# Two-part products of 256 columns merged into 512 in eight feed-forward blocks, with reordered gates in a recurrent block

## The chip, the cores and the metric

The program runs on one core of one Trainium2 chip. The metric is device time in microseconds (us) from start to end of one execution. The kernel before took 2142.56 us (median of 3 runs, 2142.15 to 2143.3).

## The reference

Thirteen blocks follow one another on a residual stream x of 256 tokens by 1024 features, batch 1: eight SwiGLU feed-forward blocks (half weight in the residual for all), one HGRN2 recurrent block, one forgetting attention, one short convolution, one shared key/value block and one sparse attention. Everything is float32. What bears on the change:

```python
def swiglu(h, w_in, w_out):                     # D_FF = 2816, eight times
    gate, up = jnp.split(h @ w_in, 2, axis=-1)
    return (jax.nn.silu(gate) * up) @ w_out

def hgrn2_mixer(h, w_in, lb, out_norm_g, w_out):
    q, z_f, i, g = jnp.split(h @ w_in, 4, axis=-1)
    f = lb + (1.0 - lb) * jax.nn.sigmoid(z32)
    k = (1.0 - lb) * jax.nn.sigmoid(-z32)
    q = jax.nn.silu(q)
    ...                                          # o: gated linear recurrence over q, k, f, v
    o = rmsnorm(o, out_norm_g).reshape(B, T, D_MODEL)
    o = o * jax.nn.silu(g)
    return o @ w_out

def short_conv_mixer(x, w_in, conv_w, w_out):
    b_gate, c_gate, v = jnp.split(x @ w_in, 3, axis=-1)
    ...                                          # y: causal convolution of c_gate * v, width 3
    return (b_gate * y) @ w_out
```

## The kernel before, in words

**Products.** Each float32 number is split in two parts of a shorter type (float32r): a high part h and a rest l. A product w·x is then wh·xh + wh·xl + wl·xh: three matmuls, each with its own load of 128x128 weights and 256 moving columns (`mm_w`, or `mm_x` where the activations are the weights). `proj` makes one product of the stream with one piece of weights: 1024 features to 256, that is 2 halves of 128 outputs by 8 steps of 128 features by 3 matmuls, 48 in all. Its two halves share one PSUM bank, which is read as 128x512. `proj_out` is the product back to the stream, also 48 matmuls, into four accumulating banks.

**Weights.** Pieces of 1 MB arrive by DMA on SP's queue into four buffers, in the order of `plan()`. `prep` casts a quarter of a piece to its high part on ScalarE (line 177) and subtracts it on VectorE for the low part (line 179); the quarters named in `pool_parts` are subtracted on GpSimd instead.

**Order.** Everything is emitted in an order written out by hand. A model clock `self.t` advances with each matmul by a fixed cost; `tick()` then emits a quarter of `prep` each `pace`, and runs a step of any background generator whose due time has come (`spawn`, `yield 3600.0`). `finish(task)` emits what remains of a generator at once. The engines execute in emission order and wait on semaphores.

**A feed-forward block** (`ffn`) has 11 units: gate product, up product, then the output product of the unit before. The gate's bank is scaled by the norm's factor on VectorE (line 477), then Silu on ScalarE (479), scaling on GpSimd (480), times the up product on VectorE (484), split into ah and al (487, 488). The first unit interleaves gate and up over the 8 feature steps (`outer`), while the previous block's last results arrive, and the norm's factor is computed in it (`stats`); `spread` then broadcasts the factor with two matmuls from dg (line 444) and a copy to rb (line 453). Only in the very first block does another product (`ahead`) stand ahead of `spread`. PSUM has 8 banks: a ring P of four for products and the other four for accumulation; in the block after the key/value block (site 10) P has three.

**The recurrent block** (`hg`) has four passes of products q, z and v; each spawns `levels`, which runs seven levels: matmuls of kk and qs into a bank, an update of qs on VectorE (568) and of kk on GpSimd (569), then a masked copy on VectorE (575). After the four passes come four gate products, then four output products. `levels` ends with a norm (squares on ScalarE, an 11-instruction root on 4 columns on VectorE, lines 414 to 425) and writes `on` (599); `gated` multiplies it on GpSimd and transposes it. From the third pass on, a pass first finishes the task of two passes before. Quarters 1 and 3 of each piece are subtracted on GpSimd.

**Convolution and tables.** In the convolution, each pass has products b, c and v in ring P. `tables` (attention bias tables for a later block: five small matmuls, two PSUM copies and DMAs on GpSimd's queue, 3 MB to DRAM) runs in the background of the third block, with banks from ring P.

Of the kernel before, what the change touches and what calls it, by code (L numbers as in the profile page):

```python
# [71 lines left out]
def plan(phases=PHASES):  # L72
# [10 lines left out]
    for ph in phases:  # L83
# [8 lines left out]
        elif ph[0] == "hg":  # L92
            for p in range(4):
                pieces += [("hg_w_in", (0,), "in", block(4 * s + p)) for s in range(3)]
            pieces += [("hg_w_in", (0,), "in", block(12 + p)) for p in range(4)]
            pieces += [("hg_w_out", (0,), "out", block(p)) for p in range(4)]
        elif ph[0] == "fox":
            pieces += [("fox_w_in", (0,), "in", block(0)), ("fox_w_in", (0,), "in", block(4))]
            pieces.append(("fox_w_in", (0,), "in", range(4096, 4112)))
            pieces.append(("fox_w_in", (0,), "in", block(8)))  # L100
            for p in range(1, 4):
                pieces += [("fox_w_in", (0,), "in", block(4 * s + p)) for s in range(3)]
            pieces += [("fox_w_in", (0,), "in", block(12 + p)) for p in range(4)]
# [15 lines left out]
class Builder:  # L119
# [154 lines left out]
    def proj(self, kinds, xs, outer=False, stats=None):  # L274
# [31 lines left out]
        return banks  # L306

    def mini(self, n, xs, ring=None):

# [35 lines left out]
    def begin_site(self, site):  # L345
        pl = self.kvx if site == 9 and self.kvx else self.act
        self.site = site
        self.xs = (
            pl.tile([128, 8, 256], F32R, name="xh", tag="xh", bufs=1),
            pl.tile([128, 8, 256], F32R, name="xl", tag="xl", bufs=1),  # L350
        )
        self.ssum = self.sm.tile([128, 512], F32, name="ssum", tag="ssum", bufs=1)
# [106 lines left out]
    def ffn(self, nxt):  # L459
        nc, tc = self.nc, self.tc  # L460
        A = self.comp(self.P + self.aside)
        xs = self.xs
        with tc.tile_pool(name="ffn", bufs=2, reuse_waits="tile") as pl:
            acc = prev = ahead = None
            for u in range(NU):
                if u == 0 and self.site != 10:
                    begin = self.use_i == 0
# [8 lines left out]
                g1 = pl.tile([128, 2, 256], F32, name="g1", tag="g1")  # L476
# [6 lines left out]
                av = pl.tile([128, 2, 256], F32, name="av", tag="av")  # L483
                nc.vector.tensor_tensor(av, banks[1].rearrange("p (c t) -> p c t", c=2), sg, op=ALU.mult)  # L484
                ah = pl.tile([128, 2, 256], F32R, name="ah", tag="ah")
# [39 lines left out]
    def hg(self, nxt):  # L525
# [3 lines left out]
        with tc.tile_pool(name="hg", bufs=2, reuse_waits="tile") as pl:  # L529
            masks = pl.tile([128, 576], F32, name="masks", tag="masks", bufs=1)  # L530
            nc.scalar.dma_start(masks, self.a["M"])
            lb8, oml = self.lb8, self.oml
            self.pool_parts = (1, 3)
            scs = [pl.tile([128, 6, 128], F32, name=f"sc{i}", tag=f"sc{i}", bufs=1) for i in range(2)]
            for s in scs:
                nc.gpsimd.memset(s, 0.0)
            on = pl.tile([128, 2, 1024], F32, name="on", tag="on", bufs=1)
            paces = (3600.0, 3600.0, 3600.0, 3000.0)
            tiles = [(j, h) for j in range(2) for h in range(2)]

            def levels(p, qs, kk, ff, v):
# [57 lines left out]
                nc.vector.tensor_tensor(  # L599
                    on[:, :, 256 * p:256 * p + 256].rearrange("p j (h d) -> p j h d", h=2),  # L600
                    o.rearrange("p (j h d) -> p j h d", j=2, h=2),
                    rs.rearrange("p (j h) -> p j h", j=2)[:, :, :, None].to_broadcast([128, 2, 2, 128]),
                    op=ALU.mult,
                )
# [7 lines left out]
            tasks = []  # L612
            for p in range(4):
                if p == 0:
                    bq, bz = self.proj("ww", xs, outer=True, stats=lambda: self.stats(True))
                    self.spread()
                else:
                    (bq,) = self.proj("w", xs)
# [20 lines left out]
                (bv,) = self.proj("x", xs)  # L639
# [4 lines left out]
            gn = self.rows[:, R_GN:R_GN + 128]  # L644
            zs, zt = {}, []
            for p in range(4):
                (bg,) = self.proj("x", xs)
                gs = pl.tile([128, 2, 256], F32, name="gs", tag="gs", bufs=3)
                for j in range(2):
                    bj = bg[:, 256 * j:256 * j + 256]  # L650
                    nc.scalar.activation(gs[:, j], bj, AF.Silu, scale=self.rn[:, j:j + 1])
                g4 = gs.rearrange("p j (h d) -> p (j h) d", h=2)
                nc.gpsimd.tensor_tensor(g4, g4, gn[:, None, :].to_broadcast([128, 4, 128]), op=ALU.mult)
                zt.append(self.spawn(gated(p, gs, zs), 1500.0))

            def z(j):
                self.finish(zt[j])
                return zs[j]
# [48 lines left out]
    def fox(self, nxt):  # L707
# [6 lines left out]
        with tc.tile_pool(name="fox", bufs=2, reuse_waits="tile") as pl:  # L714
# [6 lines left out]
            def forget(turn):  # L721
# [172 lines left out]
    def conv(self, nxt):  # L894
        nc, tc = self.nc, self.tc
        xs = self.xs
        with tc.tile_pool(name="conv", bufs=2, reuse_waits="tile") as pl:
# [4 lines left out]
            for p in range(4):  # L902
                if p == 0:
                    bb, bc = self.proj("ww", xs, outer=True, stats=lambda: self.stats(True))
                    self.spread()
                else:
                    (bb,) = self.proj("w", xs)
# [6 lines left out]
                nc.vector.tensor_tensor(c1, bc.rearrange("p (c t) -> p c t", c=2), self.rb2(), op=ALU.mult)  # L914
                (bv,) = self.proj("w", xs)
                nc.vector.tensor_tensor(v1, bv.rearrange("p (c t) -> p c t", c=2), self.rb2(), op=ALU.mult)
# [16 lines left out]
    def tables(self, pl):  # L933
# [15 lines left out]
        b = self.bank(self.P)  # L949
        for q in range(4):  # L950
# [407 lines left out]
    def run(self):  # L1358
        nc, tc = self.nc, self.tc
        ph = self.phases  # L1360
        with tc.manual_schedule():
# [206 lines left out]
```

## Time and profile before

| | |
|---|---|
| median of 3 runs | 2142.56 us |
| profiled execution, its own time | 2140.52 us |
| its span (first to last instruction) | 2138.4 us |
| mean granted TensorE clock | 0.994 of full |
| TensorE (PE) busy | 2087.5 us, 98%, 17,299 matmuls |
| VectorE (DVE) busy | 1419.4 us, 66% |
| ScalarE (ACT) busy | 1027.9 us, 48% |
| GpSimd (POOL) busy | 401.4 us, 19% |
| DMA | 368.93 MB, mean 173 GB/s |

Busy time of a matmul runs to a modelled end and overlaps the next matmul's, so a busy PE says that it did not wait, and the distance from one start to the next says how fast it went. PE is the matmul itself, PEld its weight load. By the ends of the residual additions (line 392) the first feed-forward block ends at 203.6 us, the recurrent block at 385.4, and the other blocks at 577.1, 767.6, 925.8 (forgetting attention), 1116.2, 1306.0, 1399.0 (convolution), 1589.4, then key/value and the block after it 1823.0, sparse attention 1945.2, and the last at 2135.0.

### The profile page before, as it was taken

The page shows a single profiled execution, that of the slowest core. Times are in us where ns is not written, and L with a number is a line of the kernel's source. Part 1 is how long each engine was busy: PE and PEld are TensorE (multiplying, and loading weights), DVE is VectorE, ACT ScalarE, POOL GpSimd, SP SyncE. Part 2 cuts the span into 40 slices and gives each one's busy share as a digit, 9 for nine tenths or more (in the row PEclk, how much of TensorE's full clock was granted, in tenths as well). Part 3 has the DMA queues.
Part 4 walks back from the last instruction along what each step waited for, and adds up shares of the span by engine and source line. Part 5 has one row for each costly group of instructions (what it writes and reads, how often), then busy time and mean ns, then how long its engine had stood idle before and what let it go on. Part 6 is the DMA issues. An engine that isn't in the chain of part 4 may idle for free.

```text
span 2138.4 us, 41531 instructions
## 1 busy us (share of the span) xinstructions
PE 2087.5 (98%) x17299; PEld 2064.0 (97%) x17299; DVE 1419.4 (66%) x2566; ACT 1027.9 (48%) x2076; POOL 401.4 (19%) x357
## 2 busy tenths in 40 slices
PE   8999889999999998999999999999999999999999
PEld 7999889999999998999999999999999999879999
DVE  7656776756666578575667657775578665687554
ACT  5544434544444456654454445454445444565442
POOL 2002646300100023320010001110021100442000
PEclk9999999999999999999999999999999999999999
DMA  7554423595455545345545554555546554223551
GB/s 264 199 191 149 158 80 122 181 238 196 152 205 190 175 158 183 133 175 200 178 158 207 188 179 156 200 193 181 186 174 228 179 185 170 97 101 131 211 190 60
DMA packets 57020, 368.93 MB, mean 173 GB/s; under 512 B 6318, under 2 KB 10694, under 8 KB 14080
## 3 DMA queue, kind: packets, MB, share of 16 engines
q1 hardware_dynamic: 53600, 355.49, 46.3%
q0 software_dynamic: 2656, 10.07, 2.5%
q8 instruction: 135, 2.21, 0.4%
q10 hardware_dynamic: 576, 0.72, 0.1%
q14 instruction: 53, 0.43, 0.1%
HBM read 360.75 MB, written 4.46 MB: 171 GB/s over the span
## 4 chain that ended last, share of the span: by engine, by line
PE 72%; DVE 6%; ACT 2%; issue 1%; POOL 0%; DMA 0%; DVEq 0%; ACTq 0%
PE b L245 71%; DVE wl L179 2%; PE b L250 1%; DVE xl L360 1%; ACT wh L177 1%; DVE x L392 1%; DVE rs_t L423 0%; DVE rs_t L424 0%; ACT xh L356 0%; POOL ssum L372 0%; DMA cd<-cn 0%; DVE nss L675 0%; DVE nrs L425 0%; DVE oc L1248 0%; ACT p L1193 0%
## 5 line engine op out<-in xcount | busy, mean ns | idle before, releaser
L179 DVE TENSOR_TENSOR wl<-wr,wh 128x512 fp32r<-128x512 f32 x1229 | 851.1, 751 | 247.5 <-ACT wh L177 247.3
L245 PE MATMUL b<-xh,wh 128*128 128x256 f32 x3184 | 908.3, 285 | 7.3 <-ACT wh L1430 7.3
L245 PE MATMUL b<-xh,wl 128*128 128x256 f32 x3184 | 904.9, 284 | 2.7 <-DVE wl L1431 2.7
L245 PE MATMUL b<-xl,wh 128*128 128x256 f32 x3184 | 904.4, 284 | 0.0
L177 ACT CAST wh<-wr 128x512 fp32r<-128x512 f32 x1332 | 725.3, 616 | 149.7 <-issue 132.1
L245 PEld LDWEIGHTS b<-xh,wh 128*128 128x128 f32 x3184 | 613.8, 193 | 7.5 <-ACT wh L1430 7.3
L245 PEld LDWEIGHTS b<-xh,wl 128*128 128x128 f32 x3184 | 613.5, 193 | 3.6 <-DVE wl L1431 3.6
L245 PEld LDWEIGHTS b<-xl,wh 128*128 128x128 f32 x3184 | 613.7, 193 | 0.0
L245 PE MATMUL b<-ah,wh 128*128 128x256 f32 x1408 | 394.5, 280 | 0.0
L245 PE MATMUL b<-al,wh 128*128 128x256 f32 x1408 | 394.4, 280 | 0.0
L245 PE MATMUL b<-ah,wl 128*128 128x256 f32 x1408 | 394.2, 280 | 0.0
L480 POOL TENSOR_TENSOR sg<-sg,rb 128x512 f32<-128x512 f32 x88 | 114.2, 1298 | 1245.5 <-ACT sg L479 1245.4
L245 PEld LDWEIGHTS b<-al,wh 128*128 128x128 f32 x1408 | 265.2, 188 | 0.2 <-DVE al L488 0.2
L245 PEld LDWEIGHTS b<-ah,wh 128*128 128x128 f32 x1408 | 265.2, 188 | 0.0
L245 PEld LDWEIGHTS b<-ah,wl 128*128 128x128 f32 x1408 | 264.8, 188 | 0.0
L479 ACT ACTIVATE sg<-g 128x512 f32<-128x512 f32 x88 | 55.6, 632 | 319.9 <-DVE g L477 319.9
L487 ACT CAST ah<-av 128x512 fp32r<-128x512 f32 x88 | 54.6, 621 | 259.6 <-DVE av L484 259.6
L179 POOL TENSOR_TENSOR wl<-wr,wh 128x512 fp32r<-128x512 f32 x103 | 144.2, 1412 | 163.1 <-ACT wh L177 138.7
L477 DVE TENSOR_TENSOR g<-b,rb 128x512 f32<-128x512 f32 x88 | 60.7, 690 | 170.9 <-PE b L245 169.0
L245 PE MATMUL b<-wh,xh 128*128 128x256 f32 x512 | 151.7, 296 | 5.4 <-DVE qn L686 5.4
L245 PE MATMUL b<-wl,xh 128*128 128x256 f32 x512 | 146.3, 286 | 0.0
L245 PE MATMUL b<-wh,xl 128*128 128x256 f32 x512 | 146.1, 285 | 0.0
(256 smaller groups left out, 1919.7 us busy)
## 6 DMA issues: line engine op xcount, KB each, us to landing
wr<-in_W_dram SPq DMA_DIRECT2D x332, 1024.0 KB, 4.8
td<-t POOLq DMA_DIRECT2D x1, 3072.0 KB, 37.5
wr<-in_W_dram SPq DMA_DIRECT2D x8, 256.0 KB, 6.2
bc<-cd POOLq DMA_DIRECT2D x4, 512.0 KB, 4.1
w<-in_CW_dram POOLq DMA_DIRECT2D x2, 1024.0 KB, 13.3
bt<-td SPq DMA_DIRECT2D x8, 256.0 KB, 4.3
x<-in_XT_dram SPq DMA_DIRECT2D x4, 256.0 KB, 5.7
wr<-in_W_dram SPq DMA_DIRECT2D x2, 512.0 KB, 3.8
```

The costliest lines, as they stand in the source:

```text
L177: nc.scalar.copy(h[:, s], r[:, s])
L179: eng.tensor_tensor(l[:, s], r[:, s], h[:, s].bitcast(F32), op=ALU.subtract)
L245: self.nc.tensor.matmul(out, lhsT, rhs, start=start, stop=stop, skip_group_check=True)
L250: self.nc.tensor.transpose(out, in_, self.c("ID")[:n, :n])
L360: self.nc.vector.scalar_tensor_tensor(xs[1][:, d], self.x[:, d], g, xs[0][:, d].bitcast(F32), op0=ALU.mult, op1=ALU.subtract)
L392: nc.vector.scalar_tensor_tensor(x, acc[i], factor, x, op0=ALU.mult, op1=ALU.add)
L477: nc.vector.tensor_tensor(g1, banks[0].rearrange("p (c t) -> p c t", c=2), self.rb2(), op=ALU.mult)
L479: nc.scalar.activation(sg, g1, AF.Silu)
L480: nc.gpsimd.tensor_tensor(sg, sg, self.rb2(), op=ALU.mult)
L487: nc.scalar.copy(ah, av)
```

## The change

- In `ffn` all gate and up products go through `proj_wide`: xh and xl lie side by side in one tile `xw`, so that wh·[xh, xl] is one matmul with 512 columns into a whole bank and wl·xh one with 256 into its first half. A product takes two banks, one for each half of its outputs.
- `join` adds the halves of a bank: ScalarE copies columns 256 to 511 to SBUF, VectorE adds them to columns 0 to 255; twice for a product. The scaling by the norm and the product with the gate then read SBUF.
- All blocks but site 10 do the next gate product ahead of `spread`, in the accumulation ring's banks.
- Recurrent block: the gate products stand in the passes (none, 0, 1, 2 and 3), with their weights reordered; `levels` multiplies o by the norm and the gate in four VectorE instructions of 128x128 in place of one of 128x512 and a GpSimd multiply, and makes the transposes itself; the affine steps of ff and kk go from VectorE to ScalarE; only quarter 3 goes to GpSimd; v of pass 0 stands ahead of `spread`.
- Convolution: v of pass 0 stands ahead of `spread`; `tables` runs here and takes banks outside P.
- Forgetting attention: the small tile cn no longer shares a buffer with nsq.

```diff
-                pieces += ... for s in range(3)]
-            pieces += [("hg_w_in", (0,), "in", block(12 + p)) for p in range(4)]
+                pieces += [("hg_w_in", (0,), "in", block(12 + g)) for g in ((), (0,), (1,), (2, 3))[p]]
...
+    def proj_wide(self, n, xw, outer=False, stats=None, ring=None):
+        ...
+            banks.append([self.bank(ring or self.P) for _ in range(2)])
+        def one(i, c, k):
+            h, l = ws[i]
+            b = banks[i][c]
+            s = slice(128 * c, 128 * c + 128)
+            self.mm(b[:, 0:256], l[:, k, s], xw[:, k, 0], k == 0, False, 109.0)
+            self.mm(b, h[:, k, s], xw[:, k].rearrange("p e t -> p (e t)"), False, k == 7, 218.0)
+            self.tick()
+        ...
+    def join(self, pl, out, pair):
+        lo = pl.tile([128, 2, 256], F32, name="lo", tag="lo")
+        for c in range(2):
+            nc.scalar.copy(lo[:, c], pair[c][:, 256:512])
+            nc.vector.tensor_tensor(out[:, c], pair[c][:, 0:256], lo[:, c], op=ALU.add)
...
                 if u == 0 and self.site != 10:
-                    banks = self.proj("ww", xs, outer=True, stats=lambda: self.stats(True, A))
-                    if begin:
-                        ahead = self.proj("w", xs)
+                    banks = self.proj_wide(2, xw, outer=True, stats=lambda: self.stats(True, A))
+                    self.join(pl, g1, banks[0])
+                    self.join(pl, av, banks[1])
+                    ahead = self.proj_wide(1, xw, ring=A)
                     self.spread()
-                elif ahead:
-                    banks, ahead = ahead, None
                 else:
-                    banks = self.proj("w", xs)
-                nc.vector.tensor_tensor(g1, banks[0].rearrange("p (c t) -> p c t", c=2), self.rb2(), op=ALU.mult)
+                    banks, ahead = ahead or self.proj_wide(1, xw), None
+                    self.join(pl, g1, banks[0])
+                nc.vector.tensor_tensor(g1, g1, self.rb2(), op=ALU.mult)
...
-                    banks += self.proj("w", xs)
-                nc.vector.tensor_tensor(av, banks[1].rearrange("p (c t) -> p c t", c=2), sg, op=ALU.mult)
+                    self.join(pl, av, self.proj_wide(1, xw)[0])
+                nc.vector.tensor_tensor(av, av, sg, op=ALU.mult)
...
-            self.pool_parts = (1, 3)
+            self.pool_parts = (3,)
...
-                nc.vector.tensor_tensor(on[...], o, rs, op=ALU.mult)
-            def gated(p, gs, zs):
-                yield from self.await_(tasks[p])
-                nc.gpsimd.tensor_tensor(gs, gs, on[:, :, 256 * p:256 * p + 256], op=ALU.mult)
-                yield 3000.0
+                while p not in gated:
+                    yield 300.0
+                gs = gated[p]
+                for g, (j, h) in enumerate(tiles):
+                    gg = gs[:, j, 128 * h:128 * h + 128]
+                    nc.vector.scalar_tensor_tensor(gg, o[:, 128 * g:128 * g + 128], rs[:, g:g + 1], gg, op0=ALU.mult, op1=ALU.mult)
+                yield 7000.0
                 zs[p] = self.to_feature(pl, gs, B)
...
-                    nc.vector.tensor_scalar(ff[:, h], ff[:, h], oml[:, i:i + 1], lb8[:, i:i + 1], op0=ALU.mult, op1=ALU.add)
-                    nc.vector.tensor_scalar(kk[:, h], kk[:, h], oml[:, i:i + 1], None, op0=ALU.mult)
+                    nc.scalar.activation(ff[:, h], ff[:, h], AF.Identity, bias=lb8[:, i:i + 1], scale=oml[:, i:i + 1])
+                    nc.scalar.activation(kk[:, h], kk[:, h], AF.Copy, scale=oml[:, i:i + 1])
...
-                cn = pl.tile([16, 256], F32, name="cn", tag="nsq", bufs=1)
+                cn = pl.tile([16, 256], F32, name="cn", tag="cn", bufs=1)
...
                     bb, bc = self.proj("ww", xs, outer=True, stats=lambda: self.stats(True))
+                    (bv,) = self.proj("w", xs)
                     self.spread()
...
-        b = self.bank(self.P)
+        b = self.bank(self.comp(self.P))
...
-                if i == min(2, len(ph) - 1):
+                if p[0] == "conv":
                     task = self.spawn(self.tables(...))
```

## Rows read from the trace of the kernel before

**Rows 1.** Page, part 1 (busy time) and part 4 (chain that ended last, by engine).

```profile
PE 2087.5 (98%) x17299; PEld 2064.0 (97%) x17299; DVE 1419.4 (66%) x2566; ACT 1027.9 (48%) x2076; POOL 401.4 (19%) x357
PE 72%; DVE 6%; ACT 2%; issue 1%; POOL 0%; DMA 0%; DVEq 0%; ACTq 0%
```

**Rows 2.** Windows: stretch, length, busy by engine (last row PE alone), clock, DMA, GB/s.

```profile
925.80:1116.20 190.40, 189.75 (x1594) 189.55 (x1593) 122.19 (x191) 90.66 (x169) 19.20 (x15) 1.00 0.51 183
203.60:385.40 181.80, 162.74 (x1307) 159.85 (x1306) 131.14 (x231) 73.65 (x168) 107.30 (x86) 0.96 0.33 118
...
237.30:239.30 2.00, 2.00 (x11) 0.50 0.63 266
```

**Rows 3.** Groups by line and shape in a feed-forward block, 947 to 1099 us.

```profile
L245 PE MATMUL b<-xh,wh 128*128 128x256 f32 x283 | 80.2, 283 | 0.0
...
L179 DVE TENSOR_TENSOR wl<-wr,wh 128x512 fp32r<-128x512 f32 x112 | 75.9, 739 | 24.7 <-ACT wh L177 24.7
...
L480 POOL TENSOR_TENSOR sg<-sg,rb 128x512 f32<-128x512 f32 x9 | 11.7, 1295 | 130.4 <-ACT sg L479 130.4
...
L479 ACT ACTIVATE sg<-g 128x512 f32<-128x512 f32 x9 | 5.7, 632 | 35.6 <-DVE g L477 35.6
```

**Rows 4.** Timeline of PE there: start us, duration, instruction.

```profile
1000.04 0.28 PE L245 MATMUL b<-xh,wh 128*128 128x256 f32 x1
...
1001.12 0.28 PE L245 MATMUL b<-ah,wh 128*128 128x256 f32 x1
...
1003.00 0.28 PE L245 MATMUL b<-al,wh 128*128 128x256 f32 x1
```

**Rows 5.** Timeline of PE in a stretch of half clock.

```profile
237.44 0.42 PE L245 MATMUL b<-xh,wh 128*128 128x256 f32 x1
...
239.57 0.41 PE L245 MATMUL b<-xl,wh 128*128 128x256 f32 x1
```

**Rows 6.** Timeline of PE: plain float32 matmuls at full clock, merged.

```profile
292.95 1.00 PE L245 MATMUL b<-qs,kk 128*128 128x64 f32 x8
...
1906.08 1.10 PE L245 MATMUL b<-vcz,pcT 128*128 128x256 f32 x4 [0.16 <-DVE mx L1191]
1907.02 1.23 PE L245 MATMUL b<-vv,pT 128*128 128x64 f32 x10
```

**Rows 7.** Waits of PE in the recurrent block: total, times, longest.

```profile
PE b L245 <- DVE qs L568: 12.9, 7, 4.3
PE b L245 <- DVE dg L444: 2.9, 1, 2.9
```

**Rows 8.** Groups by line and shape in the recurrent block, 204 to 385 us.

```profile
L179 POOL TENSOR_TENSOR wl<-wr,wh 128x512 fp32r<-128x512 f32 x40 | 61.5, 1548 | 16.9 <-ACT wh L177 16.9
...
L179 DVE TENSOR_TENSOR wl<-wr,wh 128x512 fp32r<-128x512 f32 x40 | 39.5, 1004 | 9.5 <-ACT wh L177 9.5
...
L608 POOL TENSOR_TENSOR gs<-gs,on 128x512 f32<-128x512 f32 x4 | 6.8, 1691 | 0.1
...
L636 DVE TENSOR_SCALAR ff<-ff,oml,lb 128x256 f32<-128x256 f32 x8 | 4.1, 518 | 3.3 <-ACT ff L632 3.3
...
L637 DVE TENSOR_SCALAR kk<-kk,oml 128x256 f32<-128x256 f32 x8 | 2.8, 347 | 0.3
...
L568 DVE TENSOR_TENSOR qs<-qs,ff 128x256 f32<-128x256 f32 x4 | 1.6, 412 | 0.0
```

**Rows 9.** Timeline at the start of the block after the convolution.

```profile
1410.86 0.71 PE L245 MATMUL b<-dg,consts 128*128 128x128 f32 x4 [0.67 <-DVE dg L444]
...
1411.61 0.37 ACT L453 COPY rb<-b 128x256 f32<-128x256 f32 x1 [6.26 <-PE b L245]
...
1412.02 0.69 DVE L477 TENSOR_TENSOR g<-b,rb 128x512 f32<-128x512 f32 x1 [0.41 <-ACT rb L453]
```

**Rows 10.** Waits of PE, 577 to 592 us; waits in the first block, 30 to 40 us.

```profile
PE b L245 <- DVE dg L444: 0.7, 1, 0.7
...
PEld b L245 <- DVE al L488: 0.2, 1, 0.2
```

More of the change, by code (lines that the diff above doesn't have):

```diff
@@ L306, in proj @@
         return banks
+    def proj_wide(self, n, xw, outer=False, stats=None, ring=None):
+        ws, banks = [], []
+        for _ in range(n):
+            h, l = self.get()
+            ws.append((h.rearrange("p (k n) -> p k n", k=8), l.rearrange("p (k n) -> p k n", k=8)))
+            banks.append([self.bank(ring or self.P) for _ in range(2)])
[6 more added lines that the diff above has]
+            self.tick()
+        if outer:
+            self.hold = False
+            for k in range(8):
+                for i in range(n):
+                    for c in range(2):
+                        one(i, c, k)
+                if k == (4 if self.use_i > 2 else 6) and stats:
+                    stats()
+            self.done(n)
+        else:
+            for i in range(n):
+                for c in range(2):
+                    for k in range(8):
+                        one(i, c, k)
+                self.done()
+        return banks
+    def join(self, pl, out, pair):
+        nc = self.nc
+        lo = pl.tile([128, 2, 256], F32, name="lo", tag="lo")
+        for c in range(2):
+            nc.scalar.copy(lo[:, c], pair[c][:, 256:512])
+            nc.vector.tensor_tensor(out[:, c], pair[c][:, 0:256], lo[:, c], op=ALU.add)
     def mini(self, n, xs, ring=None):
@@ L347, in begin_site @@
         self.site = site
[L348 to L351, printed above, removed]
+        self.xw = pl.tile([128, 8, 2, 256], F32R, name="xw", tag="xw", bufs=1)
+        self.xs = (self.xw[:, :, 0], self.xw[:, :, 1])
         self.ssum = self.sm.tile([128, 512], F32, name="ssum", tag="ssum", bufs=1)
@@ L461, in ffn @@
         A = self.comp(self.P + self.aside)
-        xs = self.xs
+        xw = self.xw
         with tc.tile_pool(name="ffn", bufs=2, reuse_waits="tile") as pl:
@@ L465, in ffn @@
             for u in range(NU):
+                g1 = pl.tile([128, 2, 256], F32, name="g1", tag="g1")
+                av = pl.tile([128, 2, 256], F32, name="av", tag="av")
                 if u == 0 and self.site != 10:
-                    begin = self.use_i == 0
-                    banks = self.proj("ww", xs, outer=True, stats=lambda: self.stats(True, A))
-                    if begin:
-                        ahead = self.proj("w", xs)
+                    banks = self.proj_wide(2, xw, outer=True, stats=lambda: self.stats(True, A))
+                    self.join(pl, g1, banks[0])
+                    self.join(pl, av, banks[1])
+                    ahead = self.proj_wide(1, xw, ring=A)
                     self.spread()
-                elif ahead:
-                    banks, ahead = ahead, None
-                else:
-                    banks = self.proj("w", xs)
-                g1 = pl.tile([128, 2, 256], F32, name="g1", tag="g1")
-                nc.vector.tensor_tensor(g1, banks[0].rearrange("p (c t) -> p c t", c=2), self.rb2(), op=ALU.mult)
+                else:
+                    banks, ahead = ahead or self.proj_wide(1, xw), None
+                    self.join(pl, g1, banks[0])
+                nc.vector.tensor_tensor(g1, g1, self.rb2(), op=ALU.mult)
                 sg = pl.tile([128, 2, 256], F32, name="sg", tag="sg")
@@ L481, in ffn @@
                 if len(banks) == 1:
-                    banks += self.proj("w", xs)
-                av = pl.tile([128, 2, 256], F32, name="av", tag="av")
-                nc.vector.tensor_tensor(av, banks[1].rearrange("p (c t) -> p c t", c=2), sg, op=ALU.mult)
+                    self.join(pl, av, self.proj_wide(1, xw)[0])
+                nc.vector.tensor_tensor(av, av, sg, op=ALU.mult)
                 ah = pl.tile([128, 2, 256], F32R, name="ah", tag="ah")
@@ L536, in hg @@
                 nc.gpsimd.memset(s, 0.0)
-            on = pl.tile([128, 2, 1024], F32, name="on", tag="on", bufs=1)
             paces = (3600.0, 3600.0, 3600.0, 3000.0)
@@ L598, in levels @@
                 self.rsqrt(ss, 128, rs, "ho", 4)
[L599 to L604, printed above, removed]
-            def gated(p, gs, zs):
-                yield from self.await_(tasks[p])
-                nc.gpsimd.tensor_tensor(gs, gs, on[:, :, 256 * p:256 * p + 256], op=ALU.mult)
-                yield 3000.0
+                while p not in gated:
[5 more added lines that the diff above has]
+                yield 7000.0
                 zs[p] = self.to_feature(pl, gs, B)
-            tasks = []
+            gn = self.rows[:, R_GN:R_GN + 128]
+            tasks, zs, gated = [], {}, {}
             for p in range(4):
@@ L615, in hg @@
                     bq, bz = self.proj("ww", xs, outer=True, stats=lambda: self.stats(True))
+                    (bv,) = self.proj("x", xs)
                     self.spread()
@@ L635, in hg @@
                     i = 2 * p + h
-                    nc.vector.tensor_scalar(ff[:, h], ff[:, h], oml[:, i:i + 1], lb8[:, i:i + 1], op0=ALU.mult, op1=ALU.add)
-                    nc.vector.tensor_scalar(kk[:, h], kk[:, h], oml[:, i:i + 1], None, op0=ALU.mult)
+                    nc.scalar.activation(ff[:, h], ff[:, h], AF.Identity, bias=lb8[:, i:i + 1], scale=oml[:, i:i + 1])
+                    nc.scalar.activation(kk[:, h], kk[:, h], AF.Copy, scale=oml[:, i:i + 1])
                 nc.vector.tensor_scalar(ff, ff, 1e-30, None, op0=ALU.max)
-                (bv,) = self.proj("x", xs)
+                if p:
+                    (bv,) = self.proj("x", xs)
                 v = pl.tile([128, 2, 256], F32, name="v", tag="v")
@@ L643, in hg @@
                 tasks.append(self.spawn(levels(p, qs, kk, ff, v), 500.0))
[L644 to L654, printed above, removed]
+                for i in ((), (0,), (1,), (2, 3))[p]:
+                    (bg,) = self.proj("x", xs)
+                    gs = pl.tile([128, 2, 256], F32, name="gs", tag="gs", bufs=3)
+                    for j in range(2):
+                        bj = bg[:, 256 * j:256 * j + 256]
+                        nc.scalar.activation(gs[:, j], bj, AF.Silu, scale=self.rn[:, j:j + 1])
+                    g4 = gs.rearrange("p j (h d) -> p (j h) d", h=2)
+                    nc.gpsimd.tensor_tensor(g4, g4, gn[:, None, :].to_broadcast([128, 4, 128]), op=ALU.mult)
+                    gated[i] = gs
             def z(j):
-                self.finish(zt[j])
+                self.finish(tasks[j])
                 return zs[j]
@@ L914, in conv @@
                 nc.vector.tensor_tensor(c1, bc.rearrange("p (c t) -> p c t", c=2), self.rb2(), op=ALU.mult)
-                (bv,) = self.proj("w", xs)
+                if p:
+                    (bv,) = self.proj("w", xs)
                 nc.vector.tensor_tensor(v1, bv.rearrange("p (c t) -> p c t", c=2), self.rb2(), op=ALU.mult)
@@ L945, in tables @@
         yield 1500.0
-        b = self.bank(self.P)
+        b = self.bank(self.comp(self.P))
         self.mm(b[0:16, 0:384], rb, oh[:, 0:384], cost=650.0)
         nc.vector.tensor_copy(t1, b[0:16, 0:384])
-        b = self.bank(self.P)
+        b = self.bank(self.comp(self.P))
         for q in range(4):
```

## The prediction

> **What bounds the kernel now.** I read the page's busy line and its chain of waits first, then windows by block, then the timeline of the matmuls, then the waits in the blocks where PE's share is low. PE is busy for 98% of the span, and 72% of the chain that ends last is PE [rows 1]; DVE, next, is busy for 66%. In a feed-forward block PE is busy for 189.75 of 190.40 us, while DVE has 122.19 and ACT 90.66 [rows 2]. So there the time is the number of matmuls times their distance from start to start. The recurrent block is different: 162.74 of 181.80 us, with DVE at 131.14, POOL at 107.30 and a mean clock of 0.96 [rows 2]. PE waits there, above all for VectorE's updates of qs: 12.9 us in seven waits, the longest 4.3 [rows 7].
>
> The step is what matters. Nine steps of gate and up matmuls from 1000.04 to 1001.12 give 0.120 us each; 16 steps of output matmuls from 1001.12 to 1003.00 give 0.1175 [rows 4]. The durations of 283 ns [rows 3] overlap and say nothing of the rate. At half clock ten steps of the same matmul take 237.44 to 239.57, or 0.213 us each [rows 5], at a clock of 0.50 [rows 2]. That is 256 columns at 1.2 GHz (0.2133) with nothing on top. At 2.4 GHz the columns alone would take 0.1067, yet 0.120 is seen: 0.013 is lost for each pair of weight load and matmul, and it is lost only where the columns take less than the pair can be turned around. A matmul with only 64 columns supports this: eight of them take 1.00 us with a last duration of 0.28, so about 0.103 a step although a quarter of the columns move [rows 6]. Something of 0.10 to 0.12 us for a pair sets the pace at full clock, and the columns of a short matmul lie beneath it.
>
> **Part by part: the wide products.** Eight blocks by 11 units by 2 products by 2 halves by 8 feature steps are 2,816 triples, each three matmuls of 0.120, or 0.360 us. After, a triple is wl·xh with 256 columns and wh·[xh, xl] with 512. The first keeps 0.120: beneath it lies the next weight load. For the second the trace has no row at full clock, so I bound it. Below: columns alone, 0.213, the same columns-time as the half-clock row, which shows nothing on top [rows 5]. Above: two present steps, 0.240. Between lie 0.226 (columns and the 0.013 once) and four plain float32 matmuls of 256 columns, each read as 0.235 at most (1906.08 to 1907.02, with the entry into the next kind in it) [rows 6]. I take 0.217, close to the half-clock row, because that is the same pair of instructions with the same time for its columns. A triple is then 0.337, 0.023 less, and 2,816 of them give 64 us. At 0.226 they give 39; with columns alone for both matmuls (0.107 + 0.213 = 0.320) they give 112.
>
> The Trainium skill (TensorE: Matmul & The Clock Gate, "Wait — 56ns, not 53.3ns?") has a fixed cost of about 2.5 ns for each matmul at full clock. By that a triple would be 3 times 0.109 now and 0.109 + 0.216 after, and the estimate of the gain is 7 us, which speaks against the change. The trace does not agree on the first: it has 0.120 in place of 0.109. The same page (LDWEIGHTS) has 128 columns of weights load in P/1.2, 107 ns, whatever the moving operand; 0.103 to 0.120 a pair is near that.
>
> **The joins.** Each product adds two ACT copies and two DVE additions of 128x256, 44 of each in a block. A 128x256 addition is 0.41 [rows 8], so DVE gets 18 us; an ACT copy of that size from PSUM is 0.37 [rows 9], 16 us. DVE goes from 122 to 140 of about 182 us, ACT from 91 to 107. PE stays the bound. What covers their latency: after a gate product the up product (5.4 us) runs, and the chain is copy 0.4, addition 0.4, scaling 0.7 [rows 8, 9], Silu 0.6, POOL 1.3 [rows 3]; after the up product the output product of the unit before (5.6 us) runs, over copy, addition, multiplication, split, about 2.8. Each bank is free two products later. The first half's join can run while the second half is computed. Behind a waiting copy on ACT's queue stand the casts of the next pieces; these are up to two pieces ahead. In site 10, with three banks, the up product's second half takes the gate's first bank, 2.7 us after the gate ended; an early join needs 0.8. So I cost the joins at nothing. If that cover were gone, the price would be what PE waits per product times 176.
>
> **Starts of blocks.** Where `spread` comes at once, PE waits 0.7 us for dg [rows 10]; three of seven starts show this. With a gate product ahead it goes, about 2 us in all. What is late next is the first unit's al: the first block, which has this order already, shows 0.2 [rows 10], over six blocks 1.2. Convolution and recurrent block move v ahead of `spread` too, but there the bank of the first product is needed next, and it is free only after the broadcast, the copy to rb and one scaling: from 1410.86 to 1412.71, 1.85 us [rows 9], of which PE waits some 1.6. That costs the convolution about 1.3 net; the recurrent block loses a wait of 2.9 [rows 7] and gains 1.6. `tables` leaves the third block, for some 0.5. Its DMAs go with it past the same POOL queue, and nothing reads them before the key/value block. cn's own buffer I cost at nothing.
>
> **The recurrent block.** POOL loses 20 of its 40 subtractions (1.548 each) and four multiplications (1.691): 38 us of 107. DVE gains 20 subtractions; at 0.74, their price where POOL is idle [rows 3], 14.8. It loses ff and kk, 6.9 [rows 8], and `on`, four times 0.7 as any 128x512 from PSUM [rows 9], and gains 16 of 128x128, of which 0.41 is the upper price and half of that near: 3 to 7. That is about +9 of work. Against it, with POOL busy a DVE subtraction takes 1.004 [rows 8] in place of 0.739 [rows 3]; 40 of them lose 11 us, other two-input operations as much, and 38/107 of this goes: about -8. So DVE's load is equal, and its chain of updates runs with fewer interruptions. ACT gets 16 affine steps at about 0.4, 6.4 us, on an engine at 74 of 182. The gate products now fill PE between levels, one in passes 1 and 2 and two in pass 3; before, they ran when most levels were over. By the model clock the first task's transposes are then forced in pass 2 about 3 us ahead of their data, and the last pass has less left to lie under: I charge 3. I expect the 12.9 of waits to fall by 8, dg by 1.3, and half of the clock loss to go (a mean clock of 0.96 [rows 2] is 0.04/0.5 of 182 us, some 14 us, at half clock, so 7 lost): 8 + 1.3 + 3 - 3, about 9, the 3 for the clock rounded down. From both sides: 18 us of the waits and the clock loss gone, or 8 us lost to a DVE queue with more of the weights in it.
>
> **Sum.** -64 (products) -9 (recurrent block) -0.8 (starts) +1.3 (convolution) -0.5 (tables) = -73, from 2140.5 of the profiled execution to 2067.5. The median of the runs is 2 us above that execution: 2069.
>
> **Rivals.**
> - *Columns alone bind (0.320 a triple).* For it: half-clock steps show no addition. Against: then the 256-column pair would lie under the neighbour's slack, and nothing in the trace shows a pair below 0.115. -112 and -9: 2021.
> - *The step is in proportion to the columns (0.240 for 512).* The 0.013 would then be something met while moving columns, or the fixed cost of 2.5 ns is all that merging can save. Against: half clock has no such share. Only the recurrent block and starts are left: about 2132. That the change doesn't do what it says would look like this.
> - *Slower: the joins hold up ACT's queue.* ACT waits at each copy for PE; the casts behind it come late, then DVE's subtractions, and PE waits for weights. 176 products; it decides from 76/176 = 0.43 us of waiting per product. At 0.6 it gives 106 - 73 = +33: 2175. For it: DVE already waits 24.7 us for casts in that stretch [rows 3]. Against: PE waits for neither there, and ACT is at 48%.
>
> **How the numbers follow.** Forecast 0.76, columns alone 0.08, in proportion 0.09, held queue 0.07. The forecast's own range is 2035 to 2108: 0.328 to 0.346 a triple, and the recurrent block from -18 to +8. Toward the first rival I go to 2020; the top, 2112, is 39 less and 8 lost. About 0.2% can be told from no change. Forecast and first rival are faster, and most of the second: 0.90; same 0.03, slower 0.07.
>
> **What would show it.** In the trace after, a pair of wl and wh steps in a feed-forward block should be 0.120 and 0.217; a block should take about 182 us, with DVE near 140. PE's wait for qs in the recurrent block should be under 5 us, and a wait of about 1.6 us should stand after `spread` there and in the convolution. A PE wait in mid-block for casts, for lo or for an addition would make the prediction wrong; so would a wide step of 0.24.

## The result, and the profile after

The changed kernel took 2120.51 us (median of 4 runs, 2117.84 to 2122.74) against 2142.78 of before (4 runs): ratio 0.9896, 95% interval 0.9879 to 0.9913. It is faster by 1.0%, a third of what was forecast (2069), and outside the stated range (2020 to 2112). The profiled execution took 2121.60, its span is 2119.6, 18.8 us less than before.

The block times, from the ends of the residual additions (us; "kv+10" is the key/value block and the feed-forward block after it), with those of the experiments that follow:

```
         before  after  narrow  block3  cn_shared  late  split  runs8_ticks  best  pool_both
ffn 0     203.6  201.6   203.7   202.4    201.9   201.5  201.3     200.5    200.8    201.6
recurrent 181.8  177.5   174.5   177.3    176.6   175.5  177.3     173.8    175.1    181.3
ffn 2     191.7  187.0   189.5   197.6    187.0   186.9  187.0     185.9    187.7    186.9
ffn 3     190.5  187.3   189.5   187.0    187.3   187.3  187.3     185.8    185.8    187.3
forget    158.2  153.1   154.4   152.9    157.0   153.1  152.9     153.1    153.2    153.2
ffn 5     190.4  187.3   189.8   187.4    187.3   187.5  187.5     186.2    186.3    187.4
ffn 6     189.8  187.3   189.5   186.9    187.3   186.9  186.9     185.8    185.8    186.9
conv       93.0  103.3   102.4    94.2    103.5   103.5   96.1     101.8     93.0    105.6
ffn 8     190.4  187.0   189.5   187.0    186.9   187.0  188.0     185.9    185.8    186.9
kv+10     233.6  232.8   235.4   231.7    232.8   232.8  232.8     231.3    230.1    232.9
sparse    122.2  124.4   123.6   122.6    122.6   124.3  124.3     121.2    121.8    122.3
ffn 12    189.8  187.6   189.8   187.6    187.6   187.6  187.7     186.3    186.3    187.7
```

The eight feed-forward blocks gained 22 us together (with the key/value block, which stands in one row with the last but one), the recurrent block 4, forgetting attention 5; the convolution lost 10, sparse attention 2. That is the 18.8 us between the two traces. In the same order the forecast had gains of 65, 9 and 0, a loss of 1.3, and 0. The busy line of the page of after, answering to [rows 1]:

```profile
PE 2071.3 (98%) x14483; PEld 1921.0 (91%) x14483; DVE 1544.3 (73%) x2934; ACT 1157.5 (55%) x2448; POOL 363.1 (17%) x333
```

There are 2,816 matmuls fewer, yet PE is busy as before. Windows of after for a feed-forward block, the recurrent block and the convolution (columns as in [rows 2]):

```profile
906.50:1093.80 187.30, 187.09 (x1243) 171.13 (x1242) 138.37 (x236) 105.21 (x213) 19.20 (x15) 1.00 0.51 186
201.60:379.20 177.60, 163.39 (x1305) 161.08 (x1304) 127.16 (x247) 86.13 (x189) 68.93 (x62) 0.95 0.34 121
1281.10:1384.40 103.30, 97.61 (x787) 96.07 (x786) 71.66 (x135) 42.30 (x82) 21.21 (x21) 0.97 0.72 198
```

In the feed-forward block PE waits for 0.2 us of 187.3; VectorE at 138 and ScalarE at 105 are where the forecast put them (140, 107), and neither holds PE up. The time is the steps. Timeline of PE of after, output matmuls and then a gate product (start, duration), answering to [rows 4]:

```profile
1000.04 0.28 PE L245 MATMUL b<-ah,wl 128*128 128x256 f32 x1
...
1002.65 0.28 PE L245 MATMUL b<-xw,wl 128*128 128x256 f32 x1
1002.76 0.40 PE L245 MATMUL b<-xw,wh 128*128 128x512 f32 x1
1003.00 0.28 PE L245 MATMUL b<-xw,wl 128*128 128x256 f32 x1
```

The narrow step takes 0.11, the wide one 0.24, together 0.35. Over the trace their medians are 0.117 and 0.233, and a block takes 187.3 us where the forecast had about 182. The 22 steps of output matmuls take 0.1186 each, before 0.1175.

The waits of PE in the recurrent block of after, answering to [rows 7]: the wait for dg is gone, one for the first bank (q) of 1.3 stands in its place, and qs fell from 12.9 to 8.9. The wait for ACT's kk is new; line 673 is an affine step that the change moved to ScalarE. The mean clock of the block is 0.95, as before (0.96).

```profile
PE b L245 <- DVE qs L606: 8.9, 6, 2.3
PE b L245 <- ACT kk L673: 2.2, 1, 2.2
PE b L245 <- POOL kk L607: 1.8, 1, 1.8
PE b L245 <- DVE q L656: 1.3, 1, 1.3
```

In the convolution of after, waits of PE, then of ACT, and a piece of the chain of waits there (start, us):

```profile
PE b L245 <- DVE c L950: 2.8, 1, 2.8
PE b L245 <- DVE v L953: 1.6, 1, 1.6
PE b L245 <- DVE b L947: 1.3, 1, 1.3
```

```profile
ACT zh L965 <- POOL y L962: 38.7, 4, 14.8
ACT wh L177 <- DMA wr<-in_W_dram: 9.6, 2, 7.7
```

```profile
1335.96 23.66 DMA wr<-in_W_dram
...
1359.72 0.63 ACT wh L177
...
1362.87 0.61 DVE v L953
```

The wait for b is the bank wait that the forecast priced at 1.6. Those for c and v come from late weights: c and v stand on VectorE's queue behind subtractions, these wait for casts, the casts for DMA, and the chain runs through a piece's landing for 23.66 us. From 1300 to 1385 us the median piece lands after 5.7 us (4.9 in the convolution of before), the 3 MB of the tables after 36.7.

### The profile page after: what moved, and what is told of

It is laid out like the page before. It is cut to its first block, busy times and chain, and to the rows that moved or that the text cites. A ratio compares the mean times of both kernels' runs of the same rounds, so it can differ in the third digit from the quotient of the medians.

```text
span 2119.6 us, 36640 instructions
## 1 busy us (share of the span) xinstructions
PE 2071.3 (98%) x14483; PEld 1921.0 (91%) x14483; DVE 1544.3 (73%) x2934; ACT 1157.5 (55%) x2448; POOL 363.1 (17%) x333
## 4 chain that ended last, share of the span: by engine, by line
PE 86%; DVE 7%; ACT 3%; DMA 2%; issue 1%; POOL 1%; ACTq 0%; SPq 0%; DVEq 0%; POOLq 0%
PE b L245 85%; DVE wl L179 2%; DMA wr<-in_W_dram 1%; PE b L250 1%; DVE xw L400 1%; ACT wh L177 0%; DVE rs_t L463 0%; DMA bc<-cd 0%; DVE rs_t L464 0%; DMA consts<-in_C_dram 0%; DVE qs L606 0%; DVE oc L1285 0%; ACT p L1230 0%; DVE nss L710 0%; DVE x L432 0%
## 5 line engine op out<-in xcount | busy, mean ns | idle before, releaser
L245 PE MATMUL b<-xw,wh 128*128 128x512 f32 (+1 forms) x3552 | 1132.1, 374 | 2.6 <-DVE b L947 1.3
L245 PE MATMUL b<-xw,wl 128*128 128x256 f32 x3184 | 898.1, 282 | 11.5 <-DVE wl L1468 10.6
L245 PEld LDWEIGHTS b<-xw,wh 128*128 128x128 f32 x3552 | 646.6, 190 | 124.6 <-issue 2.9
L245 PEld LDWEIGHTS b<-xw,wl 128*128 128x128 f32 x3184 | 604.7, 190 | 13.0 <-DVE wl L1468 11.5
L346 ACT COPY lo<-b 128x256 f32<-128x256 f32 x352 | 127.0, 371 | 279.6 <-PE b L245 279.6
L245 PE MATMUL b<-wh,xw 128*128 128x256 f32 x1024 | 201.3, 290 | 1.4 <-DVE qn L721 1.4
L347 DVE TENSOR_TENSOR g<-b,lo 128x256 f32<-128x256 f32 x176 | 72.3, 422 | 144.2 <-ACT lo L346 144.0
L245 PEld LDWEIGHTS b<-wh,xw 128*128 128x128 f32 x1024 | 165.6, 193 | 3.0 <-issue 2.4
L245 PE MATMUL b<-wl,xw 128*128 128x256 f32 x512 | 145.7, 285 | 0.0
L527 DVE TENSOR_TENSOR al<-av,ah 128x512 fp32r<-128x512 f32 x88 | 61.0, 693 | 60.5 <-ACT ah L526 60.5
## 6 DMA issues: line engine op xcount, KB each, us to landing
td<-t POOLq DMA_DIRECT2D x1, 3072.0 KB, 36.7
```

What stands on the lines that cost most here:

```text
L245: self.nc.tensor.matmul(out, lhsT, rhs, start=start, stop=stop, skip_group_check=True)
L346: nc.scalar.copy(lo[:, c], pair[c][:, 256:512])
L347: nc.vector.tensor_tensor(out[:, c], pair[c][:, 0:256], lo[:, c], op=ALU.add)
L527: nc.vector.tensor_tensor(al, av, ah.bitcast(F32), op=ALU.subtract)
```

## Experiments

**1. The step of a matmul by itself** (`steps`: the blocks are replaced by streams of one shape; one run).

> This kernel leaves the network out: after the first weights and the first split of x it runs streams of matmuls on PE alone, each stream 40 to 150 matmuls of one shape, with VectorE, ScalarE and DMA idle; only x is written out. Read: start-to-start step of each stream. Theory 'pair' (a fixed loss for each pair of weight load and matmul): float32r 512 columns 0.226, 384 0.173, 256 0.120; triple 3 x 256 0.360, triple 256 + 512 0.346. Theory 'columns' (a loss in proportion): 512 columns 0.240, 384 0.180, 256 0.120, triple 256 + 512 0.360. Theory 'neighbours' (the loss comes from what the other engines and DMA read and write): 0.107 and 0.213 plus some 0.003, since they idle here. If the weight load makes it, half a weight load (64 columns of weights) halves the loss on 512 columns: about 0.220. If it is of float32r, bf16 shows 0.216 for 512.

Measured, from the timeline (first and last of a stretch, or a merged row):

```profile
134.81 0.28 PE L245 MATMUL rtwo<-xw,wh 128*128 128x256 f32 x1
...
135.89 0.28 PE L245 MATMUL rtwo<-xw,wl 128*128 128x256 f32 x1
...
114.69 0.33 PE L245 MATMUL rthree<-xw,wh 128*128 128x384 f32 x1
...
115.91 0.33 PE L245 MATMUL rthree<-xw,wl 128*128 128x384 f32 x1
...
94.64 0.39 PE L245 MATMUL rfive<-xw,wh 128*128 128x512 f32 x1
...
96.00 0.39 PE L245 MATMUL rfive<-xw,wh 128*128 128x512 f32 x1
...
79.78 0.51 PE L245 MATMUL wide<-xw,wh 128*128 128x512 f32 x2
...
81.19 0.40 PE L245 MATMUL wide<-xw,wh 128*128 128x512 f32 x1
...
214.76 0.28 PE L245 MATMUL halfwtwo<-xw,wl 128*64 128x256 f32 x1
...
215.89 0.28 PE L245 MATMUL halfwtwo<-xw,wl 128*64 128x256 f32 x1
...
229.63 2.11 PE L245 MATMUL bfive<-x,w 128*128 128x512 bf16 x9
...
149.82 0.27 PE L245 MATMUL rone<-xw,wh 128*128 128x128 f32 x1
...
150.94 0.28 PE L245 MATMUL rone<-xw,wh 128*128 128x128 f32 x1
```

256 columns: 9 steps in 1.08, 0.120. 384: 7 in 1.22, 0.174. 512: 6 in 1.36, 0.227. Each is its columns at 2.4 GHz plus some 0.013, so theory "pair" holds for these widths, "columns" falls (0.240 for 512), and so does "neighbours": with the other engines idle the step is the same 0.120. With 128 columns a step is 0.112 (10 in 1.12) and not the 0.067 of columns plus 0.013; so short matmuls do stand at a floor, as the prediction had it for 64. The 0.013 is of float32r: bf16 with 512 columns takes (2.11 - 0.38)/8 = 0.216, and the plain float32 stream `ftwo` with 256 columns has a median of 0.216 too. With 64 columns of weights, 256 moving columns fall to 0.113 (10 steps in 1.13), but 512 did not fall (mean 0.230), so what the weight load has to do with it stays open. And a thing no theory had: narrow and wide in turns take 4 pairs in 1.41, 0.353, not 0.120 + 0.227 = 0.347.

**2. The merge alone** (`narrow`).

```diff
-            self.mm(b, h[:, k, s], xw[:, k].rearrange("p e t -> p (e t)"), False, k == 7, 218.0)
+            self.mm(b[:, 0:256], h[:, k, s], xw[:, k, 0], False, False, 109.0)
+            self.mm(b[:, 256:512], h[:, k, s], xw[:, k, 1], False, k == 7, 109.0)
```

> The kernel after with one line undone: in proj_wide wh x [xh, xl] is two matmuls of 256 columns again, into the same two halves of the bank; joins, order, banks and all else stay. Theory 'a wide step saves about 0.010 a triple': 2,816 triples slower by 28 us, 2149. Rival 'the merge saves nothing and the gain of after comes from elsewhere': 2120. Had the predicted 0.217 held anywhere, it would be 64 us: 2184.

2138.47 (11 runs), 0.9988 of before (0.9979 to 0.9997); after's ratio is 0.9896. The merge is worth some 18 to 20 us: 2.1 to 2.6 in each feed-forward block, by the table. That is less than the 28 expected. In this kernel the steps of a triple have a median of 0.120, so a triple is 0.360 there and 0.349 to 0.351 in after; 352 times 0.010 is 3.5 a block, and 0.5 to 0.8 of it goes back through the block's 528 output matmuls, which take 0.119 in after, 0.1175 to 0.118 in `narrow` and before. Against before, `narrow` has all the joins, and its blocks are as long (the first and the last) or 0.3 to 1.0 shorter (2.2 in the third, which has no tables): there the joins cost nothing that can be seen. The exception is kv+10, 1.8 longer, where ring P has three banks: PE waits 0.9 for ACT's vv ahead of the first wide product, which before does not have, and 0.9 for dg in place of 0.3.

**3. Tables in the third block again** (`tables_block3`).

```diff
-                if p[0] == "conv":
+                if i == 2:
...
-        b = self.bank(self.comp(self.P))
+        b = self.bank(self.P)
```

> The kernel after with the tables task in the third block again (banks from ring P), convolution otherwise as after. Theory 'the tables' 3 MB of small DMA packets delay weight pieces in the convolution': the convolution falls from 103 to about 95 us, the third block rises by 1 to 2, whole 2113. Rival 'the convolution lost its time to v ahead of spread': convolution still 103, whole 2120 or a little above.

2118.56, ratio 0.9888 (0.9874 to 0.9901). The convolution falls to 94.2 as expected, but the third block rises by 10.6, not by 1 to 2. PE waits there 3.9 us at the tables' first matmul and then runs at half clock (0.50 from 422 to 426 us). VectorE's timeline shows why; the tables' step stands behind nine subtractions:

```profile
411.66 5.50 DVE L179 TENSOR_TENSOR wl<-wr,wh 128x512 fp32r<-128x512 f32 x9
417.08 0.15 DVE L980 TENSOR_SCALAR rbx<-rbx 32x16 f32<-32x16 f32 x1
```

```profile
417.45 1.43 PE L245 MATMUL b<-oh,rbx 33*16 33x384 f32 x2 [3.91 <-issue]
...
422.05 0.41 PE L245 MATMUL b<-xw,wl 128*128 128x256 f32 x1
...
425.89 0.41 PE L245 MATMUL b<-xw,wl 128*128 128x256 f32 x1
```

Six triples take 3.84 us here, 0.640 each: 768 columns at 1.2 GHz, with nothing on top for the wide matmul either.

The tables' DMAs did no harm in this block: PE waits for no weights.

**4. cn in nsq's buffer** (`cn_shared`).

```diff
-                cn = pl.tile([16, 256], F32, name="cn", tag="cn", bufs=1)
+                cn = pl.tile([16, 256], F32, name="cn", tag="nsq", bufs=1)
```

> The kernel after with cn in nsq's buffer again. Theory 'the shared buffer held up the norm of forgetting attention': the block goes from 153 to 158 us, whole 2125. Rival 'the 5 us there come from other timing': 153, whole 2120.

2123.14, ratio 0.9917 (0.9904 to 0.9931); its interval meets that of after, but the block moves from 153.1 to 157.0, and ACT shows the wait, which after does not have (first the trace of before, then `cn_shared`):

```profile
802.57 0.60 ACT L674 ACTIVATE nsq<-b 128x512 f32<-128x512 f32 x1 [5.99 <-DMA cd<-cn]
...
ACT nsq L709 <- DMA cd<-cn: 4.8, 1, 4.8
```

So the separate buffer is worth 4 of the 5 us.

**5. When and how many bytes** (`tables_late`, `tables_split`). In the first, `yield 1500.0` ahead of the tables' DMAs became `yield 12000.0`. In the second:

```diff
-        nc.gpsimd.dma_start(self.td, t1[:, None, :].to_broadcast([16, 128, 384]))
+        nc.gpsimd.dma_start(self.td[:, 0:8], t1[:, None, :].to_broadcast([16, 8, 384]))
...
+        yield 90000.0
+        nc.gpsimd.dma_start(self.td[:, 8:128], t1[:, None, :].to_broadcast([16, 120, 384]))
```

> The kernel after with the tables' DMAs emitted 10.5 us of model clock later, so that they stand behind the convolution's next multiply on GpSimd's queue. Theory 'GpSimd's queue was blocked: the DMAs waited there for their table ahead of u, so u, y and zh came late, and behind zh on ScalarE the weight casts': convolution falls from 103 to about 95, whole 2112. Rival 'the 3 MB themselves slow the weight pieces': convolution stays near 103.

> The kernel after with 8 of the 128 copies of the table (and the four small DMAs) written at the same place and the other 120 at the end of the convolution. Theory 'blocked queue alone': nothing changes, convolution 103. Rival 'bytes alone': convolution about 94, and some of it in the block after. Both needed: the stretch without weight casts (1318 to 1329 us) stays, but the late piece does not: convolution about 95.

Late: 2119.03, ratio 0.9896 (0.9880 to 0.9913), the convolution still 103.5, although u and y now pass ahead of the DMAs; ACT's wait for weights is even longer:

```profile
ACT wh L177 <- DMA wr<-in_W_dram: 12.1, 2, 6.8
```

Split: 2114.82, ratio 0.9871 (0.9857 to 0.9886), convolution 96.1 and the block after it 188.0, 1.0 more than in after, with GpSimd's queue blocked as in after. So my theory of the blocked queue fell: it is the bytes. Why they harm the convolution and not the third block is argued from the trace of after and not tried: its casts come in groups, because zh waits up to 14.8 us for y at the head of ACT's queue, so pieces would be asked for late.

**6. Order of widths** (`orders`, `runs8`, `runs8_ticks`).

> Leaves the network out as the kernel 'steps' did: streams of float32r matmuls on PE alone. There 512 columns took 0.227 a step and 256 took 0.120, but the two in turns 0.353 together, 0.006 more than their sum. Theory 'a change of width costs': with the same matmuls in runs of 2, 4 and 8 the sum per pair falls towards 0.347 (0.350, 0.3485, 0.3475). Rival 'the mix of two rates costs the same in any order': 0.353 throughout. Theory 'the 0.013 is the weight load's': it shrinks with the columns of weights (64 gave 0.1135 for 256 columns); 32 columns give about 0.110 for 256 and 0.217 for 512. Rival 'it is the moving side': 32 columns give what 64 gave, 0.1135 and 0.230.

Timeline (one run): in turns five pairs from 39.91 to 41.68, 0.354; in runs of two, eight pairs from 70.99 to 73.78, 0.349; of four, 12 from 100.33 to 104.54, 0.351; of eight, eight from 126.46 to 129.26, 0.350.

```profile
39.91 0.53 PE L245 MATMUL turns<-xw,wl 128*128 128x512 f32 x2
...
41.68 0.51 PE L245 MATMUL turns<-xw,wh 128*128 128x512 f32 x2
...
70.99 0.39 PE L245 MATMUL twos<-xw,wh 128*128 128x512 f32 x1
...
73.78 0.39 PE L245 MATMUL twos<-xw,wh 128*128 128x512 f32 x1
...
100.33 0.28 PE L245 MATMUL fours<-xw,wh 128*128 128x256 f32 x1
...
104.54 0.28 PE L245 MATMUL fours<-xw,wl 128*128 128x256 f32 x1
...
126.46 0.28 PE L245 MATMUL eights<-xw,wl 128*128 128x256 f32 x1
...
129.26 0.28 PE L245 MATMUL eights<-xw,wh 128*128 128x256 f32 x1
```

So widths strictly in turns are the slowest, by 0.002 to 0.005 a pair. But the sum does not fall with the number of changes, as the theory had it (0.350, 0.3485, 0.3475), and within runs of eight a wide step still takes 0.231 in place of 0.227. That a change of width costs is therefore not shown; that both widths in one stream cost is. With 32 columns of weights 256 gave 0.113 and 512 gave 0.2315, as with 64: the weight theory fell. In the kernel (the edit of `runs8_ticks`):

```diff
-            self.mm(b[:, 0:256], l[:, k, s], xw[:, k, 0], k == 0, False, 109.0)
-            self.mm(b, h[:, k, s], xw[:, k].rearrange("p e t -> p (e t)"), False, k == 7, 218.0)
-            self.tick()
+            if part == 0:
+                self.mm(b, h[:, k, s], xw[:, k].rearrange("p e t -> p (e t)"), k == 0, False, 218.0)
+            else:
+                self.mm(b[:, 0:256], l[:, k, s], xw[:, k, 0], False, k == 7, 109.0)
+            self.tick()
...
+                    for part in range(2):
+                        for k in range(8):
+                            one(i, c, k, part)
```

> The kernel after with the order inside a wide product changed: for a half, eight matmuls of 512 columns, then the eight of 256 (in the interleaved first unit four and four). Same work, same banks. Theory 'a change of width costs 0.003 to 0.006': 2,816 triples give -8 to -17 us, 2103 to 2112. Rival 'any order costs the same': 2120.

2578.45: a miss of the experiment. There `tick()` stood in the `else` branch, so that weight quarters were emitted too rarely, and PE waited for casts (between 400 and 600 us):

```profile
PE b L245 <- ACT wh L177: 17.2, 7, 2.5
```

> The order of the kernel 'runs8' (for a half eight matmuls of 512 columns, then eight of 256), with the background pump called after every matmul; in 'runs8' it was called after the narrow ones alone, and too few weight quarters were emitted. Theory 'a change of width costs': the isolated streams gave 0.353 a triple in turns and 0.346 in runs of eight, so a feed-forward block falls by 352 x 0.004 to 0.007, 1.4 to 2.5 us, and the whole by 11 to 20, to 2100 to 2109. Rival 'order costs nothing in the kernel, where other engines run': 2120.

2103.91, ratio 0.9831 (0.9817 to 0.9844). A feed-forward block falls by 1.1 to 1.5 us, at or below the low end of what was expected (the 0.346 there for runs of eight was not what the stream showed, 0.350), and the whole by 17. The blocks make up 10 of it; the rest is in the recurrent block, the convolution and sparse attention, whose times move by 2 to 4 us between kernels in which they are the same. So some 10 us can be put down to the order. From the timeline of PE, a product and then output matmuls:

```profile
1000.35 2.00 PE L245 MATMUL b<-xw,wh 128*128 128x512 f32 x8
1002.19 1.11 PE L245 MATMUL b<-xw,wl 128*128 128x256 f32 x8
1003.14 2.00 PE L245 MATMUL b<-xw,wh 128*128 128x512 f32 x8
...
1005.93 0.28 PE L245 MATMUL b<-ah,wh 128*128 128x256 f32 x1
...
1011.45 0.28 PE L245 MATMUL b<-ah,wl 128*128 128x256 f32 x1
```

A triple is 0.349 (eight in 2.79), the wide step 0.230, and 47 steps of output matmuls take 0.1174, as in before. Over the sixth block the mean triple falls from 0.3506 to 0.3492, 0.5 us in 352, and the mean output step from 0.1189 to 0.1176, 0.7 us in 528. More than half of the gain is thus in matmuls whose own order did not change.

**7. GpSimd's share in the recurrent block** (`pool_both`: `self.pool_parts = (1, 3)`).

> The kernel after with quarters 1 and 3 of each piece on GpSimd again in the recurrent block. Theory of the prediction (the move is even for VectorE's load and shortens its waits): recurrent block 3 to 6 us longer than the 177 of after, 2123 to 2127. Rival 'VectorE was the loser by the move': 3 to 6 us shorter, 2114 to 2117.

2124.15, ratio 0.9916 (0.9902 to 0.9929). The recurrent block takes 181.3 against 177.5, as the theory has it, but its time spreads by as much in other kernels, the intervals of the two ratios meet, and 2.3 us of the difference stand in the convolution. PE's waits there, with kk at 4.4 in place of 1.8:

```profile
PE b L245 <- DVE qs L606: 9.4, 7, 3.3
PE b L245 <- POOL kk L607: 4.4, 4, 2.2
```

**8. Together** (`best`: experiment 6's order, the tables in the third block, in banks of P, with `yield 8000.0` between their VectorE step and the matmuls, the convolution's v behind `spread`).

> The kernel after with that order, the tables in the third block again with 8 us of model clock between their VectorE step and their matmuls, and the convolution's v behind spread as before. Theory: order -11 to -20; convolution at 93 in place of 103; third block at 188 to 189 less the order's gain: 2090 to 2100. Rival: the tables' bytes cost the third block what they cost the convolution: 2105 to 2112.

2096.83 (2096.32 to 2097.33), ratio 0.9791 (0.9778 to 0.9804): 2.1% below before, and below after. The convolution is back at 93.0, the third block takes 187.7, 1.9 above its neighbours.

## Why the prediction was wrong

**The wide product is the step that failed.** "I take 0.217, close to the half-clock row" had a gain of 64 us; the runs showed 0.227 for a wide step in its own stream, 0.233 to 0.24 beside narrow ones, and 18 to 20 us for the whole merge. The reading that led there was wrong: that half clock shows no addition was taken to mean that the loss lies beneath long columns. It lies on top of a float32r matmul's columns at full clock, some 0.013 for 256, 384 and 512 alike; only at 128 columns and fewer does a floor of 0.11 hide the columns. (The 64-column step, read as 0.103 from a merged row, has a median of 0.112 in the trace of before.) I had the right stream step in the sum as 0.226 and 39 us and put it at the edge. From 39 to the measured gain the rest is the mix of widths: a triple of 0.351 in place of 0.346 takes back some 15 us in 2,816, and output matmuls slower by 0.0013 some 5 in 4,224. No row of before has two widths in turns.

The Trainium skill (TensorE: Matmul & The Clock Gate, "Wait — 56ns, not 53.3ns?") has 2.5 ns on top of a matmul's columns at full clock; the bf16 stream agrees (0.216 for 512), float32r does not (0.227). The rival worked out beside that rule, 2132 with no gain from the merge, was nearer to the result on the products than the forecast; but the merge did gain.

**Tables**: priced at -0.5, they were the second failure, 8 us the wrong way with half-clock stretches in it. I looked for readers of the tables, not for whom their bytes meet: weight pieces that the convolution needs soon. Of the convolution's +10.3, v ahead of `spread` is 1.2 (94.2 against 93.0 without the tables), as forecast (1.3).

**cn**: priced at nothing, worth 4 us in the forgetting block. The wait stood in ACT's queue in the trace of before; PE's waits alone did not name it.

**Recurrent block**: -9 forecast, -4 measured in this trace, -4 to -8 over all traces of the same code. Two terms failed: the waits for qs were to fall by 8, to under 5 us, and fell by 4.0, to 8.9; half of the clock loss was to go, and the mean clock stayed (0.96, then 0.95). A wait of 2.2 for ACT's kk came, which the sum did not have. The direction held, and DVE's load did stay even (131 to 127). That fewer subtractions on GpSimd shorten the waits is not shown apart from the rest: without that move the waits were 9.4 for qs and 4.4 for kk, against 8.9 and 1.8, within a block time that is not clear of its spread.

**Joins and starts**: right but for kv+10. No PE wait in mid-block of the others, DVE 138, ACT 105; the wait for dg went where the order changed, and the bank wait behind `spread` came (1.3 in both places by the view of waits, 1.6 forecast). In kv+10, where a gain like the other blocks' was expected, 0.8 us is all that the change gained.

## What to carry to other kernels

Price a matmul by its own fixed part: measure two widths and take the intercept, for the type at hand, before counting on a wider one; a stream on an idle core does it in one run. Then measure the mix too: two widths in one stream were slower than their own streams added up, and least so in runs. When a background task moves, look at how soon its new host needs its own transfers.

## What the runs showed that was not expected

A float32r matmul at full clock costs 0.013 us above its columns for 256, 384 and 512 columns, bf16 0.003; at half clock none is seen, for 256 or 512. Fewer columns of weights (64 or 32) halve it for 256 moving columns and not for 512. The two widths in turns take 0.353 a pair, 0.006 more than their own streams; in runs of two, four and eight 0.349 to 0.351, in no order with the number of changes. Output matmuls of one width, in streams of 48, took 0.119 where the products between them had widths in turns and 0.1175 where these had one width or runs of eight. What makes these is open.
